# Grouping the output products of two recurrences by the part of the array they use, with one accumulation per PSUM bank and head pair

## The chip, the cores and the metric

The kernel runs on one core of one Trainium2 chip. The metric is device time in microseconds (us) of one execution. Before the change three runs gave a median of 1396.98 us (1395.22 to 1398.71).

## The reference, cut to what matters

The model has two layers, each a mixer and a SwiGLU feed-forward part, over 512 tokens of width 1024 in float32. The mixer of the first layer holds both recurrences of the title: RWKV-7 (8 heads of 64) and gated linear attention, GLA (4 heads, keys of 64, values of 128). The second layer's mixer is attention; it is not touched.

```python
def rwkv7_recurrence(r, w, k, v, a, b):
    def step(S, inp):
        r_t, w_t, k_t, v_t, a_t, b_t = inp
        sa = jnp.einsum('bhvk,bhk->bhv', S, a_t)
        S = S * w_t[:, :, None, :] + sa[..., None] * b_t[:, :, None, :] + v_t[..., None] * k_t[:, :, None, :]
        return S, jnp.einsum('bhvk,bhk->bhv', S, r_t)
...
def gla_chunked(q, k, v, log_a):                 # chunks of 64 tokens
...
    o_intra = jnp.einsum('bhncs,bhnse->bhnce', jnp.where(causal, scores, 0.0), v)
...
    o_inter = jnp.einsum('bhncd,nbhde->bhnce', q_dec, S_prev)
    return (o_intra + o_inter).reshape(Bsz, H, T, dv)
```

Both are computed chunk by chunk: a token's output is a sum of what comes from its own chunk of 64 tokens and what comes from the state S at the start of that chunk.

## The kernel before

Everything is kept transposed, channels on partitions and the 512 tokens in the free dimension. The large projections are done in three float32r matmuls each (`mm3`, L99 to L101); the matrices of the recurrences are plain float32, and each such product stands in the trace as two PE records, here called passes. The tile framework orders the instructions of each engine when the program is built; nothing is reordered at run time except what the engines do themselves.

GLA (`gla`). For each of 4 heads one PSUM bank `po` holds 128 value channels by 512 tokens. For each of 4 pairs of chunks (128 tokens) L398 multiplies v by the masked scores: 128 rows of the array (contraction over the pair's 128 tokens) and 128 columns. For each of 7 chunks (the first has no state) L402 adds S times the decayed queries: contraction over 64 key channels, so 64 rows and 128 columns. In the profile the two carry `128*128` and `64*128`. They are issued pair by pair: one L398, then the one or two L402 of that pair. Then ACT squares the bank (L406), PE sums (L410), ACT and DVE form the inverse root, PE spreads it (L416). Between the heads stand pieces of the first RWKV projections as filler.

RWKV (`rwkv_out`). A chunk of 128 channels is two heads; there are four of them (c = 0 to 3), and below they are called blocks, to keep them apart from chunks of tokens. Each is a generator, and `interleave` steps the generators in turn, the next one starting five steps after the last. A block does: triangular solves (L620, L627, L634), Gram products (L655, L657), state increments (L668), then the state recurrence: six steps of one PE product (L677) and one DVE addition (L678), then the output. The output bank `py` takes, for each of 8 token chunks and each of the 2 heads, L687 (contraction over 128, output to 64 partitions: `128*64`) and, except for the first chunk, L690 (contraction over 64 rows of that head, output to the same 64 partitions: `64*64`). The order is L687, L690 for the first head, L687, L690 for the second, then the next chunk: 16 of the one and 14 of the other per block. Then ACT squares and scales the bank (L692, L695), PE sums the squares (L700), ACT takes the root (L702), PE adds the gate product (L709, L710), ACT spreads the inverse root into `rb` (L705), PE transposes it (L714), DVE and POOL finish. The products L677 work on the whole array (`128*128`).

A second solve, for the last block alone, runs on DVE beside blocks 0 and 1: pairs L594 and L596, a transposition (L598), and copies by ACT (L603). The output projection of the GLA half (`mm3` into `pd`) is filler between the blocks.

Of the kernel before, what the change touches and what calls it, by code (L numbers as in the profile page):

```python
# [16 lines left out]
P = 128  # L17
# [38 lines left out]
def bank(g, use="pb"):  # L56
    use = use if use in g.pbufs else "pb"
    return g.ps.tile([P, 512], F32, name=use, bufs=g.pbufs[use])


def dbank(g):
    return bank(g, "pd")
# [41 lines left out]
def form_a(g, out, src, hi, lo):  # L104

    nk = src.shape[-1] // P
    step = g.wn // P
    k0 = 0
    while k0 < nk:
        n = min(step, nk - k0)  # L110
        if nk - k0 > n and nk - k0 < 2 * n:
            n = (nk - k0 + 1) // 2
        whi, wlo = load_split(g, src[:, k0 * P:(k0 + n) * P])
        for i in range(n):
            s = slice(i * P, i * P + P)
            mm3(g.nc, out, whi[:, s], wlo[:, s], hi[:, k0 + i], lo[:, k0 + i], k0 + i == 0, k0 + i == nk - 1)
        k0 += n
# [107 lines left out]
CH = 64  # L225
NQ = T // CH
# [89 lines left out]
def gla(g, m0, gp, v, tail, tailw, ob):  # L316

    nc, ap = g.nc, g.ap
    one = gp.tile([P, 1], F32, name="one", bufs=1)
    nc.vector.memset(one, 1.0)  # L320
    eps = gp.tile([P, 1], F32, name="eps5", bufs=1)
    nc.vector.memset(eps, 1e-5)
    dv = gp.tile([P, 1], F32, name="dv", bufs=1)
    nc.vector.memset(dv, 1.0 / P)

    def flat(t):
        return t.rearrange("p q t -> p (q t)")

    qd, ki, kx, eb, en, kd = ({} for _ in range(6))
    for j in range(2):  # L330
        pz = bank(g)
        nc.tensor.matmul(pz, lhsT=tailw[32:48, j * P:j * P + P], rhs=tail[32:48], start=True, stop=True)
        z = gp.tile([P, T], F32, name="z")
        cb = g.cols["gla_ba"] + j
        nc.scalar.activation(z, pz, AF.Identity, bias=g.vec[:, cb:cb + 1])
        e = gp.tile([P, T], F32, name="e")
        nc.vector.scalar_tensor_tensor(e, z, -1.0, z, op0=ALU.mult, op1=ALU.max)
        nc.scalar.activation(e, e, AF.Exp, scale=-1.0)
        nc.scalar.activation(e, e, AF.Ln, bias=one)
        nc.vector.scalar_tensor_tensor(e, z, 0.0, e, op0=ALU.min, op1=ALU.subtract)  # L340
        L = gp.tile([P, NQ, CH], F32, name="L")
        nc.vector.tensor_tensor_scan(flat(L), m0.reset, e, 0.0, ALU.mult, ALU.add)
        kd[j] = gp.tile([P, NQ, CH], F32, name="kd")
        nc.gpsimd.tensor_tensor(kd[j], L[:, :, CH - 1:CH].broadcast_to([P, NQ, CH]), L, op=ALU.subtract)
        eb[j] = gp.tile([P, NQ, CH], F32, name="eb")
        nc.scalar.activation(eb[j], L, AF.Exp, scale=1.0 / 16)
        en[j] = gp.tile([P, NQ, CH], F32, name="en")
        nc.scalar.activation(en[j], L, AF.Exp, scale=-1.0 / 16)
        nc.scalar.activation(kd[j], kd[j], AF.Exp, scale=1.0 / 16)
    for j in range(2):  # L350
        pq, pk = dbank(g), dbank(g)
        form_a(g, pk, ap["win"][14 + j], g.xhi, g.xlo)
        form_a(g, pq, ap["win"][12 + j], g.xhi, g.xlo)
        kx[j] = gp.tile([P, T], F32, name="kx")
        nc.vector.tensor_mul(kx[j], pk, g.rstd)
        ki[j] = gp.tile([P, T], F32, name="ki")
        nc.gpsimd.tensor_mul(ki[j], kx[j], flat(en[j]))
        nc.vector.tensor_mul(kx[j], kx[j], flat(kd[j]))
        qd[j] = gp.tile([P, T], F32, name="qd")
        nc.vector.tensor_mul(qd[j], pq, g.rstd)  # L360
        nc.vector.scalar_tensor_tensor(qd[j], qd[j], 0.125, flat(eb[j]), op0=ALU.mult, op1=ALU.mult)
    S, sc = {}, {}
    for j in range(2):
        pt = bank(g)
        for m in range(4):
            nc.tensor.transpose(pt[:, m * P:m * P + P], kx[j][:, m * P:m * P + P], g.ident)
        kt = gp.tile([P, 4, P], F32, name="kt")
        nc.scalar.copy(kt.rearrange("p m f -> p (m f)"), pt)
        for hp in range(2):
            rows = slice(64 * hp, 64 * hp + 64)  # L370
            psc = bank(g)
            for m in range(4):
                s = slice(m * P, m * P + P)
                nc.tensor.matmul(psc[:, s], lhsT=ki[j][rows, s], rhs=qd[j][rows, s], start=True, stop=True)
            sc[j, hp] = gp.tile([P, 4, P], F32, name="sc", bufs=4)
            nc.vector.tensor_tensor(sc[j, hp], psc.rearrange("p (m t) -> p m t", m=4),
                                    m0.lmask.unsqueeze(1).broadcast_to([P, 4, P]), op=ALU.mult)
        S[j] = gp.tile([P, NQ, P], F32, name="S")
        nc.gpsimd.memset(S[j][:, 0], 0.0)
        pkv = []  # L380
        for e in range(2):
            pkv.append(bank(g).rearrange("p (m d) -> p m d", m=4))
            r = slice(64 * e, 64 * e + 64)
            for m in range(4):
                for hp in range(2):
                    h = 2 * j + hp
                    nc.tensor.matmul(pkv[e][64 * hp:64 * hp + 64, m], lhsT=kt[r, m, 64 * hp:64 * hp + 64],
                                     rhs=v[r, m, h * P:h * P + P], start=True, stop=True)
        for q in range(NQ - 1):
            nc.vector.scalar_tensor_tensor(S[j][:, q + 1], S[j][:, q], eb[j][:, q, CH - 1:CH], pkv[q % 2][:, q // 2],  # L390
                                           op0=ALU.mult, op1=ALU.add)
    for h in range(4):
        j, hp = h // 2, h % 2
        rows = slice(64 * hp, 64 * hp + 64)
        po = bank(g)
        for m in range(4):
            s = slice(m * P, m * P + P)
            nc.tensor.matmul(po[:, s], lhsT=v[:, m, h * P:h * P + P], rhs=sc[j, hp][:, m], start=True, stop=False)  # L398
            for q in (2 * m, 2 * m + 1):
                if q:  # L400
                    t = slice(q * CH, q * CH + CH)
                    nc.tensor.matmul(po[:, t], lhsT=S[j][rows, q], rhs=qd[j][rows, t], start=False, stop=q % 2 == 1)  # L402
        o = gp.tile([P, T], F32, name="o")
        cn = g.cols["gla_norm"] + h
        sq = gp.tile([P, T], F32, name="sq")
        nc.scalar.activation(sq, po, AF.Square)  # L406
        nc.scalar.mul(o, po, g.vec[:, cn:cn + 1])
        pc = bank(g)
        for b in range(4):
            nc.tensor.matmul(pc[:, b:b + 1], lhsT=sq[:, b * P:b * P + P], rhs=dv, start=True, stop=True)  # L410
        rn = gp.tile([P, 4], F32, name="rn")
        nc.scalar.activation(rn, pc[:, :4], AF.Sqrt, bias=eps)
        nc.vector.reciprocal(rn, rn)
        pr = bank(g)
        for b in range(4):
            nc.tensor.transpose(pr[:, b * P:b * P + P], rn[:, b:b + 1].broadcast_to([P, P]), g.ident)  # L416
        nc.vector.tensor_mul(o, o, pr)
        nc.sync.dma_start(ob[h], o)
# [187 lines left out]
def rwkv_out(g, m0, st, sp, c, zeros):  # L606

    nc = g.nc
    use = f"o{c % 2}"
    no, G = zeros[c % 2]  # L610
    for e in range(2):
        rows = slice(64 * e, 64 * e + 32)
# [30 lines left out]
    qt = sp.tile([P, T], F32, name="qt", bufs=2)  # L643
# [3 lines left out]
    for e in range(2):  # L647
        er = slice(64 * e, 64 * e + 64)
        pe = bank(g, use).rearrange("p (x m f) -> p x m f", x=2, f=CH)
        for m in range(4):  # L650
            q = 2 * m + e
            for hp in range(2):
                ih, i = m // 2, 2 * (m % 2) + hp
                hr = slice(64 * hp, 64 * hp + 64)
                nc.tensor.matmul(pe[hr, 0, m], lhsT=st.r[er, ih, c, i, CH:], rhs=st.bk[er, c, q, hr],  # L655
                                 start=True, stop=True)
                nc.tensor.matmul(pe[hr, 1, m], lhsT=st.r[er, ih, c, i, CH:], rhs=st.gr[er, e, ih, c, i],  # L657
                                 start=True, stop=True)
        for hp in range(2):
            hr = slice(64 * hp, 64 * hp + 64)  # L660
# [3 lines left out]
    for q in range(NQ):  # L664
        m, e = q // 2, q % 2
        for hp in range(2):
            hr = slice(64 * hp, 64 * hp + 64)
            nc.tensor.matmul(ph[hr, q], lhsT=st.bk[:, c, q, hr], rhs=st.fv[:, e, m // 2, c, 2 * (m % 2) + hp],  # L668
                             start=True, stop=True)
    H = sp.tile([P, NQ, CH], F32, name="H", bufs=2)  # L670
    nc.scalar.copy(H, ph)
    S = sp.tile([P, NQ, CH], F32, name="S", bufs=2)
# [7 lines left out]
    py = bank(g, use)  # L680
    for q in range(NQ):
        m, e = q // 2, q % 2
        t = slice(q * CH, q * CH + CH)
        for hp in range(2):
            ih, i = m // 2, 2 * (m % 2) + hp
            hr = slice(64 * hp, 64 * hp + 64)
            nc.tensor.matmul(py[hr, t], lhsT=st.fv[:, e, ih, c, i], rhs=st.gr[:, e, ih, c, i],  # L687
                             start=True, stop=q == 0)
            if q:
                nc.tensor.matmul(py[hr, t], lhsT=S[hr, q], rhs=qt[hr, t], start=False, stop=True)  # L690
    sq = sp.tile([P, T], F32, name="sq", bufs=1)
    nc.scalar.activation(sq, py, AF.Square)  # L692
    y = sp.tile([P, T], F32, name="y", bufs=2)
# [14 lines left out]
    s = slice(c * P, c * P + P)  # L708
# [493 lines left out]
```

## Time and profile before

| | |
|---|---|
| median of 3 runs | 1396.98 us |
| profiled execution | 1397.71 us, span 1395.9 us |
| PE busy | 1358.7 us, 97% of the span, 6868 records |
| DVE, ACT, POOL busy | 699.9, 563.8, 185.5 us |
| mean granted PE clock | 0.969 of full speed |

Where in the span: GLA's outputs stand from 90.8 to 119.6 us, the RWKV blocks' outputs between 286.2 and 374.6 us, and from 420 us on there are only the feed-forward parts and the attention layer. A timeline row gives start and length; since consecutive passes overlap in the array, the time a row costs is the distance from its start to the start of the row behind it. The clock column reads 1.00 at 2.4 GHz and 0.50 at 1.2 GHz.

### The profile page before, as it was taken

What the parts mean: (1) busy time and instruction counts of PE and PEld (TensorE: products, weight loads), DVE (VectorE), ACT (ScalarE), POOL (GpSimd) and SP (SyncE); (2) the same over time, 40 slices, a digit from 0 to 9 for tenths busy, and PEclk for the clock granted to TensorE, in tenths of its full rate; (3) what the DMA queues carried; (4) which work ended last, traced back from release to release, by engine and by line L of the source; (5) the groups of instructions that cost most, each with busy time, mean ns of one, the idle gap of its engine ahead of it and who ended that gap; (6) DMA issues with size and microseconds to landing.
All of it is one profiled execution on the core that took longest, in us unless ns stands there. A gap on an engine that the chain in (4) does not pass through costs nothing.

```text
span 1395.9 us, 17759 instructions
## 1 busy us (share of the span) xinstructions
PE 1358.7 (97%) x6868; PEld 1111.0 (80%) x6868; DVE 699.9 (50%) x1223; ACT 563.8 (40%) x949; POOL 185.5 (13%) x167
## 2 busy tenths in 40 slices
PE   8999999799999999999999999999999999999996
PEld 6788777688787888888888888888888888888885
DVE  7563869843255343343434327898643433344332
ACT  6534774422244232222323436777532322233232
POOL 3011111200141111001111100000111110011111
PEclk9999999868799999999999999999999999999998
DMA  6122222402264432333323432221223323432231
GB/s 191 59 74 63 77 69 90 142 8 76 92 219 142 152 98 72 107 113 94 102 74 93 124 91 76 62 61 46 76 91 105 91 75 99 118 102 91 78 95 69
DMA packets 50848, 131.11 MB, mean 94 GB/s; under 512 B 5859, under 2 KB 6243, under 8 KB 50764
## 3 DMA queue, kind: packets, MB, share of 16 engines
q1 hardware_dynamic: 49900, 128.81, 30.6%
q8 instruction: 54, 0.88, 0.3%
q10 hardware_dynamic: 864, 1.17, 0.2%
q14 instruction: 30, 0.25, 0.1%
HBM read 121.22 MB, written 11.36 MB: 95 GB/s over the span
## 4 chain that ended last, share of the span: by engine, by line
PE 90%; DVE 6%; ACT 2%; issue 1%; DMA 0%; DVEq 0%; ACTq 0%
PE pd L100 24%; PE pd L101 24%; PE pd L99 24%; PE po L1001 1%; PE o L687 1%; PE o L690 1%; PE o L634 1%; PE o L627 1%; DVE wlo L89 1%; PE sc L976 1%; PE sc L977 1%; DVE tmp L594 1%; PE pb L402 1%; PE o L620 1%; PE o L101 1%
## 5 line engine op out<-in xcount | busy, mean ns | idle before, releaser
L88 ACT CAST whi<-wraw 128x1024 fp32r<-128x1024 f32 (+2 forms) x248 | 215.6, 871 | 545.8 <-PE pd L100 339.4
L101 PE MATMUL pd<-xhi,wlo 128*128 128x512 f32 x1064 | 421.2, 396 | 0.0
L99 PE MATMUL pd<-xhi,whi 128*128 128x512 f32 x1064 | 420.1, 395 | 0.9 <-ACT xhi L180 0.9
L100 PE MATMUL pd<-xlo,whi 128*128 128x512 f32 x1064 | 420.2, 395 | 0.0
L89 DVE TENSOR_TENSOR wlo<-wraw,whi 128x1024 fp32r<-128x1024 f32 (+2 forms) x248 | 256.3, 1036 | 143.9 <-ACT whi L88 143.4
L99 PEld LDWEIGHTS pd<-xhi,whi 128*128 128x128 f32 x1064 | 201.0, 189 | 42.7 <-ACT xhi L180 1.3
L100 PEld LDWEIGHTS pd<-xlo,whi 128*128 128x128 f32 x1064 | 201.2, 189 | 41.7 <-issue 0.2
L101 PEld LDWEIGHTS pd<-xhi,wlo 128*128 128x128 f32 x1064 | 201.2, 189 | 41.2 <-DVE wlo L89 0.2
L215 POOL TENSOR_TENSOR hlo<-h,hhi 128x512 fp32r<-128x512 f32 x44 | 66.7, 1516 | 547.4 <-ACT hhi L214 547.4
L100 PE MATMUL pd<-hlo,whi 128*128 128x512 f32 x352 | 136.9, 389 | 0.0
L99 PE MATMUL pd<-hhi,whi 128*128 128x512 f32 x352 | 136.9, 389 | 0.0
L101 PE MATMUL pd<-hhi,wlo 128*128 128x512 f32 x352 | 136.9, 389 | 0.0
L211 DVE TENSOR_TENSOR ut<-pd,rstd 128x512 f32<-128x512 f32 x44 | 30.4, 691 | 147.1 <-PE pd L101 147.1
L208 DVE TENSOR_TENSOR gt<-pd,rstd 128x512 f32<-128x512 f32 x44 | 30.4, 691 | 124.5 <-PE pd L101 122.4
L101 PEld LDWEIGHTS pd<-hhi,wlo 128*128 128x128 f32 x352 | 66.1, 188 | 13.8
L99 PEld LDWEIGHTS pd<-hhi,whi 128*128 128x128 f32 x352 | 66.1, 188 | 13.8
L100 PEld LDWEIGHTS pd<-hlo,whi 128*128 128x128 f32 x352 | 66.1, 188 | 13.6
L221 DVE TENSOR_TENSOR xT<-pd,xT 128x512 f32<-128x512 f32 x32 | 22.1, 691 | 67.3 <-PE pd L101 67.3
L149 POOL TENSOR_TENSOR ssum<-nsq,ssum 128x512 f32<-128x512 f32 x26 | 37.2, 1430 | 81.7 <-ACT nsq L145 81.4
L981 ACT ACTIVATE s<-s,mn 128x384 f32<-128x384 f32 (+3 forms) x64 | 35.7, 559 | 21.4 <-DVE mn L978 20.8
L214 ACT CAST hhi<-h 128x512 fp32r<-128x512 f32 x44 | 27.4, 623 | 37.1 <-DVE h L213 37.1
L957 POOL TENSOR_TENSOR qst<-q,qst 64x512 fp32r<-64x512 f32 x8 | 12.9, 1611 | 168.0 <-DVE qst L955 168.0
(327 smaller groups left out, 1686.1 us busy)
## 6 DMA issues: line engine op xcount, KB each, us to landing
wraw<-in_gate SPq DMA_DIRECT2D x44, 512.0 KB, 3.7
wraw<-in_up SPq DMA_DIRECT2D x44, 512.0 KB, 3.6
wraw<-in_down SPq DMA_DIRECT2D x32, 384.0 KB, 3.1
wraw<-in_win SPq DMA_DIRECT2D x40, 256.0 KB, 2.7
wraw<-in_down SPq DMA_DIRECT2D x32, 320.0 KB, 2.9
wraw<-in_wqk SPq DMA_DIRECT2D x16, 512.0 KB, 3.7
xT<-in_xT SPq DMA_DIRECT2D x16, 256.0 KB, 3.6
wraw<-in_wout SPq DMA_DIRECT2D x16, 256.0 KB, 3.9
```

What stands on the lines that cost most here:

```text
L88: nc.scalar.copy(hi, raw)
L89: nc.vector.tensor_sub(lo, raw, hi.bitcast(F32))
L99: nc.tensor.matmul(out, lhsT=lhi, rhs=rhi, start=start, stop=False)
L100: nc.tensor.matmul(out, lhsT=lhi, rhs=rlo, start=False, stop=False)
L101: nc.tensor.matmul(out, lhsT=llo, rhs=rhi, start=False, stop=stop)
L149: (nc.vector if c in fast else nc.gpsimd).tensor_add(ss, sq, first if c == 1 else ss)
L208: nc.vector.tensor_mul(gt, pg, rstd)
L211: nc.vector.tensor_mul(ut, pu, rstd)
L214: nc.scalar.copy(hhi[:, n], h)
L215: nc.gpsimd.tensor_sub(hlo[:, n], h, hhi[:, n].bitcast(F32))
L221: nc.vector.tensor_add(g.xT[:, j], pd, g.xT[:, j])
L981: nc.scalar.activation(s[:, m, :L], s[:, m, :L], AF.Exp, bias=mn[:, m:m + 1], scale=-1.0, accum_out=sm[:, m:m + 1])
```

## The change

Both outputs issue the same products into the same banks in another order: first all that don't read S, then all that do. The flags follow: `start` on the first product of a bank (in the RWKV case of each head's half of it), `stop` on the last.

```diff
         po = bank(g)
         for m in range(4):
             s = slice(m * P, m * P + P)
-            nc.tensor.matmul(po[:, s], lhsT=v[:, m, h * P:h * P + P], rhs=sc[j, hp][:, m], start=True, stop=False)
-            for q in (2 * m, 2 * m + 1):
-                if q:
-                    t = slice(q * CH, q * CH + CH)
-                    nc.tensor.matmul(po[:, t], lhsT=S[j][rows, q], rhs=qd[j][rows, t], start=False, stop=q % 2 == 1)
+            nc.tensor.matmul(po[:, s], lhsT=v[:, m, h * P:h * P + P], rhs=sc[j, hp][:, m], start=m == 0, stop=False)
+        for q in range(1, NQ):
+            t = slice(q * CH, q * CH + CH)
+            nc.tensor.matmul(po[:, t], lhsT=S[j][rows, q], rhs=qd[j][rows, t], start=False, stop=q == NQ - 1)
...
             nc.tensor.matmul(py[hr, t], lhsT=st.fv[:, e, ih, c, i], rhs=st.gr[:, e, ih, c, i],
-                             start=True, stop=q == 0)
-            if q:
-                nc.tensor.matmul(py[hr, t], lhsT=S[hr, q], rhs=qt[hr, t], start=False, stop=True)
+                             start=q == 0, stop=False)
+    for q in range(1, NQ):
+        t = slice(q * CH, q * CH + CH)
+        for hp in range(2):
+            hr = slice(64 * hp, 64 * hp + 64)
+            nc.tensor.matmul(py[hr, t], lhsT=S[hr, q], rhs=qt[hr, t], start=False, stop=q == NQ - 1)
```

On PE, one GLA head before (the first; L398 reads scores `sc` and `v`, L402 reads queries `qd` and state `S`):

```order
L387 MATMUL pb<-v,kt 64x128 x16
L398 MATMUL pb<-sc,v 128x128
L402 MATMUL pb<-qd,S 128x64
L398 MATMUL pb<-sc,v 128x128
L402 MATMUL pb<-qd,S 128x64 x2
L398 MATMUL pb<-sc,v 128x128
```

The same head on PE with the change (L401 is the line that was L402):

```order
L387 MATMUL pb<-v,kt 64x128 x16
L398 MATMUL pb<-sc,v 128x128 x4
L401 MATMUL pb<-qd,S 128x64 x7
L100 MATMUL pd<-xlo,whi 128x512
L101 MATMUL pd<-xhi,wlo 128x512
```

The products of one kind stand together; the projection's matmuls behind them keep their place.

On PE, the start of the last block's output before (`gr`, `xT`: the products without S; `qt`, `S`: those with it; `G`: the recurrence step):

```order
L101 MATMUL pd<-xhi,wlo 128x512
L99 MATMUL pd<-xhi,whi 128x512
L677 MATMUL o_3189<-S,G_2486 128x64
L687 MATMUL o_3192<-gr,xT 64x64 x3
L690 MATMUL o_3192<-qt,S 64x64
L687 MATMUL o_3192<-gr,xT 64x64
```

The same block on PE with the change (line numbers behind L402 shift by one or two: L676 was L677, L686 was L687, L692 was L690):

```order
L101 MATMUL pd<-xhi,wlo 128x512
L99 MATMUL pd<-xhi,whi 128x512
L676 MATMUL o_3189<-S,G_2486 128x64
L686 MATMUL o_3192<-gr,xT 64x64 x16
L692 MATMUL o_3192<-qt,S 64x64 x14
L100 MATMUL pd<-xlo,whi 128x512
```

Thirty products that changed kind at almost each step became two runs.

On PE, block 0's output before, around the end, where other blocks' work is woven in (`bkt`: state increments of block 1; `r`, `ga`: the first solve of block 2):

```order
L668 MATMUL o_2714<-xT,bkt 64x64 x16
L687 MATMUL o_2741<-gr,xT 64x64
L690 MATMUL o_2741<-qt,S 64x64
...
L687 MATMUL o_2741<-gr,xT 64x64
L620 MATMUL o_2781<-r,ga 128x128 x3
L677 MATMUL o_2738<-S,G_2486 128x64
L690 MATMUL o_2741<-qt,S 64x64
```

The same place on PE with the change:

```order
L686 MATMUL o_2741<-gr,xT 64x64 x16
L692 MATMUL o_2741<-qt,S 64x64 x2
L667 MATMUL o_2714<-xT,bkt 64x64 x16
L692 MATMUL o_2741<-qt,S 64x64 x10
L619 MATMUL o_2781<-r,ga 128x128 x3
L676 MATMUL o_2738<-S,G_2486 128x64
L692 MATMUL o_2741<-qt,S 64x64 x2
```

The work of the other blocks is woven in at the same places; within the block's own products only the order changed.

No engine issues an instruction more or fewer. On SP some 35 transfers around the output projection (weights, parts and the reload of xT) change places with each other, and DVE and ACT follow with their weight splits.

## Rows read from the trace of the kernel before

**Rows 1.** Busy time by stretch, core 0: engines, then granted clock, DMA share, GB/s.
```profile
289.80:313.30 23.50, 23.50 (x121) 18.61 (x122) 7.86 (x26) 7.47 (x12) 0.15 (x1) 0.50 0.05 12
...
323.90:334.00 10.10, 10.10 (x49) 8.59 (x48) 1.14 (x3) 2.66 (x5) 0.00 (x0) 0.50 0.37 115
...
347.80:354.30 6.50, 6.50 (x33) 5.04 (x34) 0.21 (x1) 2.73 (x7) 1.27 (x1) 0.50 0.02 3
...
354.30:371.70 17.40, 17.36 (x183) 12.82 (x180) 7.98 (x20) 4.79 (x10) 2.57 (x2) 0.99 0.24 77
371.70:381.80 10.10, 10.10 (x33) 6.68 (x32) 0.20 (x1) 2.06 (x4) 1.26 (x1) 0.50 0.54 182
sum 95.60, PE 95.56 PEld 73.73 DVE 31.50 ACT 24.78 POOL 8.46; mean PE 11.94 PEld 9.22 DVE 3.94 ACT 3.10 POOL 1.06
```

**Rows 2.** Chain of waits, 286.2 to 374.6 us, shares by line.
```profile
by line: PE o L687 19.8%; PE o L690 19.7%; PE o L620 8.6%; PE o L627 6.4%; PE o L634 6.1%; PE o L677 5.6%; PE o L710 4.6%; PE o L668 4.6%; PE o L700 4.2%; PE o L709 4.2%; PE o L655 3.1%; PE pd L101 2.3%; PE o L714 2.2%; PE o L657 2.1%; PE p
```

**Rows 3.** Timeline of PE, block outputs: start, length, line, output, rows*columns of the array.
```profile
290.10 0.47 PE L687 MATMUL o<-gr,xT 128*64 128x64 f32 x2
...
366.58 0.33 PE L690 MATMUL o<-qt,S 64*64 64x64 f32 x2
366.84 0.33 PE L687 MATMUL o<-gr,xT 128*64 128x64 f32 x2
...
374.18 0.47 PE L690 MATMUL o<-qt,S 64*64 64x64 f32 x2
374.58 0.79 PE L100 MATMUL pd<-xlo,whi 128*128 128x512 f32 x1
```

**Rows 4.** Timeline of PE, runs of one tile shape.
```profile
177.08 1.14 PE L565 MATMUL pb<-xT,ga 64*64 64x64 f32 x30
...
290.90 1.97 PE L668 MATMUL o<-xT,bkt 128*64 128x64 f32 x32
...
358.69 1.15 PE L668 MATMUL o<-xT,bkt 128*64 128x64 f32 x32
```

**Rows 5.** Timeline of PE, recurrence step L677 between two kinds of neighbours.
```profile
279.25 0.35 PE L677 MATMUL o<-S,G 128*128 128x64 f32 x2
279.42 2.16 PE L634 MATMUL o<-w,ga 128*128 128x128 f32 x8
...
283.18 0.43 PE L677 MATMUL o<-S,G 128*128 128x64 f32 x2
283.54 0.34 PE L655 MATMUL o<-bkt,r 64*64 64x64 f32 x4
```

**Rows 6.** Timeline of PE, second GLA head.
```profile
102.56 0.43 PE L402 MATMUL pb<-qd,S 64*128 64x64 f32 x2
102.92 0.49 PE L398 MATMUL pb<-sc,v 128*128 128x128 f32 x2
103.34 0.66 PE L402 MATMUL pb<-qd,S 64*128 64x64 f32 x4
103.93 0.49 PE L398 MATMUL pb<-sc,v 128*128 128x128 f32 x2
```

**Rows 7.** Busy time by stretch, behind the first GLA head.
```profile
95.50:102.00 6.50, 6.50 (x21) 5.33 (x21) 0.87 (x2) 2.58 (x4) 0.00 (x0) 0.50 0.01 3
```

**Rows 8.** Timeline of DVE and ACT, end of the second solve; PE behind it.
```profile
304.91 1.25 DVE L598 STREAM_TRANSPOSE xt<-xl 128x1024 f32<-128x1024 f32 x1
...
308.09 0.62 ACT L705 COPY rb<-rn 128x512 f32<-128x512 f32 x1
...
311.94 1.06 PE L714 MATMUL o<-ident,rb 128*128 128x128 f32 x4
```

**Rows 9.** DMA issues on the page: KB each, us to landing.
```profile
wraw<-in_wout SPq DMA_DIRECT2D x16, 256.0 KB, 3.9
```

## The prediction

> **What bounds the kernel now.** I read the busy time by stretch first, since the change touches two short places only. In the 95.6 us from 286.2 to 381.8 PE is busy for 95.56 [rows 1]: what PE saves there, the kernel saves, until another engine is late. DVE is busy for 31.5 and ACT for 24.8 of it. The same rows show a second thing: four stretches, 50.2 us together, stand at a granted clock of 0.50, the lower of its two levels. Then the chain of waits over 286.2 to 374.6: L687 and L690 hold 39.5% of 88.4 us, so 34.9 us for 120 products [rows 2]. Then the timeline: at the upper level a product that follows one of the other kind costs 0.26 us (366.58 to 366.84), at the lower one 0.40 (374.18 to 374.58) [rows 3].
>
> What such a product should cost stands in the runs of one shape. L668 has the shape of L687, alternates between the same two halves of the columns, and does 32 passes in 1.15 us, 0.036 a pass; L565 has the shape of L690 and does 30 in 1.14, 0.038 a pass [rows 4]. So two passes cost 0.07 in a run and 0.26 in the alternation: 0.19 is the price of a switch. That it is the shape and not the accumulation onto a region just written is shown by L677, which accumulates onto nothing: two passes cost 0.17 among neighbours of its own shape (279.25 to 279.42) and 0.36 among 64*64 ones (283.18 to 283.54) [rows 5]. The difference is again 0.19.
>
> **The change part by part.** No instruction is added or taken away; only PE's order matters.
>
> GLA heads. One L398 and two L402 take 102.92 to 103.93, 1.01 us. Four passes of L402 take 0.59 (103.34 to 103.93) and two 0.36 (102.56 to 102.92), so a pass in a run costs 0.115, and six of them 0.69 [rows 6]. The pair of switches costs 0.32. Three such pairs go per head, the switch from the four L398 to the seven L402 stays: 0.95 per head, **3.8 us** for four.
>
> Block outputs. A grouped output is 32 passes at 0.036, 28 at 0.038 and one switch of 0.19: 2.4 us, 9.6 for four. Where other blocks' work is woven in, a run is cut: in block 0 by L667 and by L619 with L676, in block 1 by L676, in block 2 by transposes and by solves; about ten more switches, 1.9 us. So 34.9 become 11.5: **23.4 us**. Bounds: nothing off if the blocks keep their switches elsewhere, 25 if the cuts are free.
>
> The clock. Each of the four stretches at 0.50 begins inside an alternating output and lasts into the work behind it [rows 1]. About 40 of the 120 products stand at the spacing of 0.40, the first at 290.10 and the last at 374.18 [rows 3]: 16 us of the 50.2. The other 34.2 us are solves, gates and projection at half speed. The same work costs less at the upper level: L668 takes 1.15 there and 1.97 here [rows 4], 0.58 of the time; the levels themselves stand 2 to 1, and I take 0.55, since passes with more columns wait less for weights. If the falls go with the alternation, 45% of 34.2 is **15.4 us**. The 6.5 us at 0.50 behind the first GLA head [rows 7] give **2.9 us** in the same way. No row shows what the clock does after a grouped output; the bounds are 0 and 20.4 (half of 40.7). I take a value near the upper one, because L668's run, the nearest row in shape, is dense (0.036 a pass), and because what is at 0.50 today follows alternation in all five places.
>
> What is late next. With PE faster, its order makes it wait for others. The place is block 0's transposes of `rb` (L714, today at 311.94 [rows 8]). PE's work up to there is 25.7 us today, 9.4 of it outputs; at the upper level 16.3 x 0.55 = 9.0, and 3.2 for the output with its cuts: reached at 286.2 + 12.2 = 298.4. DVE has 7.9 us of work in that stretch [rows 1]; some 4 us of it are the last solve steps and the state's additions, in turn with PE's steps, behind a copy of the state that can start at about 289.5. I let them take 6, to 295.8. The transposition L598, the three copies of ACT and the spread L705 then follow one another; today from 304.91 to 308.71, 3.8 us [rows 8]. So `rb` is there at 299.6, and PE waits 1.2 us. I add as much again for the other blocks, where squares and copies stand between PE's steps: **minus 2.5 us**, bounds 0 and 10 (if every block waits twice as long).
>
> Costed at nothing: SP's new order. Transfers take 54% of the DMA engines' time in the stretch where they bunch [rows 1], and the weights are held three tiles ahead. If that cover is gone, one late tile costs at most its landing time of 3.9 us [rows 9]. That S of the last chunk must be there is no new wait: its product was the last of the bank before as well.
>
> A rule that speaks against the change: the two heads' L692 now stand next to each other, with different halves of the rows and one bank. The trace has that case: L565 alternates between the two halves of the rows and writes one bank, to different partitions, at 0.038 a pass [rows 4]. The Trainium skill, TensorEngine Tiling (Array Packing), section Gotcha 1: PSUM Pressure, says that different row tiles cannot access the same PSUM bank at the same time. By the rule the 28 passes would stand one behind the other; by the row they don't, and the sum goes by the row.
>
> Sum: 3.8 + 23.4 + 15.4 + 2.9 - 2.5 = 43.0 us. The profiled execution took 1397.7 (its span of 1395.9 and 1.8 around it), so 1354.7; it lies 0.7 above the median, which makes **1354 us**.
>
> **The rivals.**
> 1. The falls of the clock stay, since PE's work behind the outputs (sums of squares with two columns, solves) is thin too. For it: block 0's stretch at 0.50 lasts 23.5 us, through such work. Against it: the same kinds of work stand at 0.99 between 354.3 and 371.7 [rows 1]. Then only 3.8 + 23.4 come, 1370; with the outputs at the lower level as well (0.062 a pass, so 18.9 for four in place of 11.5) 1377.
> 2. Waits take the place of the work: the solve on DVE and the chain of squares, root and spread on ACT bound each block. Each has 8 us or less of work in the longest stretch [rows 1], so it takes the 10 us of the bound above: 1362.
> 3. Passes that differ in the half of the rows don't overlap. The nearest row for passes on one half is L402's 0.115 [rows 6]: 28 x (0.115 - 0.038) = 2.2 us per block, 8.6 in all: 1363. This is what the Trainium skill's rule above would do.
> 4. The switch is not what costs, and the order gives nothing: 1397. Against it stand rows 3 to 5.
> 5. Slower: PE, no longer filled by the alternation, waits so often that the clock stays at 0.50 over the whole stage. Of the 60.7 us that are no outputs 26.5 are at the upper level now; they would become 48, the 34.2 stay, and the outputs take 18.9: 101 for 95.6. The three later GLA heads (three times 1.01 and a first pair, 3.7 us, now) would take 5.0: together 9 us more, 1406. Against it: 45.4 us of the stage are at the upper level now, with waits in their midst. It decides from about four fifths of the work at the lower level.
>
> **How the numbers follow.** Forecast 0.62, rival 1 0.20, rival 2 0.09, rival 3 0.04, rival 4 0.03, rival 5 0.02. The forecast's own range is 1347 (no cuts, no waits, all that is at 0.50 in half its time: 3.8 + 25.3 + 20.4 off) to 1363. The range of 1345 (by the 2 us that the runs lie below their median) to 1373 takes in rivals 2 and 3 and half of rival 1; some 0.17 is left out. Faster by over 0.3% (what a measurement can tell here from no change, 4 us): 0.95; within: 0.03; slower: 0.02.
>
> **What would show it.** Right: L398 and L401 of a head in some 2.7 us without an L398 between L401; sixteen L686 in 1.2 us and fourteen L692 in 1.1, neighbours 0.07 apart; no stretch at 0.50 that begins inside an output; 286.2 to 381.8 shrunk from 95.6 to about 59; from 420 us on, nothing but a shift. Wrong: the clock still falls behind the outputs (rival 1); PE idle before L716, L702 or L633 for more than a few us (rival 2); L692 spaced at 0.2 (rival 3). The forecast is wrong if the stage shrinks by less than 30 us.

## The result, and the profile after

The changed kernel takes 1354.1 us (median of 4 runs, 1350.58 to 1354.56) against 1397.2 (median of 4 runs beside it): ratio 0.9687, 95% interval 0.9667 to 0.9707. The forecast was 1354. The profiled execution took 1354.56 us, with a span of 1352.8; PE is busy for 1314.1 us of it, 44.6 less than before, and DVE, ACT and POOL for within 1.2 us of what they were.

Busy time by stretch, columns as in [rows 1]: GLA's outputs; the 13 us ahead of block 0's output and through most of it; the rest of the blocks; what follows.

```profile
90.80:113.90 23.10, 23.10 (x154) 20.64 (x152) 5.98 (x14) 6.73 (x12) 0.00 (x0) 0.93 0.18 57
272.70:286.00 13.30, 13.30 (x156) 12.02 (x158) 7.47 (x24) 1.92 (x6) 0.00 (x0) 0.50 0.01 1
286.00:338.90 52.90, 51.40 (x618) 41.32 (x614) 27.87 (x74) 24.53 (x48) 7.82 (x6) 1.00 0.31 95
338.90:400.00 61.10, 60.20 (x266) 47.66 (x266) 33.29 (x44) 29.29 (x45) 21.18 (x15) 1.00 0.54 173
```

The four stretches at 0.50 of [rows 1] (called falls of the clock below) are gone: from 286 us to the end of the blocks, and on to 400, the clock is at its upper level. One stretch of 13.3 us at 0.50 remains; it begins before block 0's output. Shorter ones stood ahead of the blocks in the kernel before too, where no output alternates:

```profile
211.20:214.50 3.30, 3.30 (x10) 2.55 (x9) 1.79 (x7) 0.86 (x3) 0.00 (x0) 0.50 0.28 82
255.60:262.30 6.70, 5.42 (x25) 5.45 (x26) 4.42 (x7) 4.51 (x8) 2.65 (x2) 0.50 0.33 98
265.80:269.20 3.40, 3.40 (x18) 3.40 (x17) 3.18 (x6) 0.89 (x3) 1.74 (x2) 0.50 0.91 263
279.50:282.80 3.30, 3.30 (x21) 2.99 (x21) 2.05 (x7) 1.33 (x4) 0.00 (x0) 0.50 0.00 0
```

From the first output to the last transposes the blocks took 96.1 us (286.24 to 382.38), and now 57.5 (281.36 to 338.85).

The chain of waits over 281.4 to 338.9 us, against [rows 2]:

```profile
by line: PE o L692 8.2%; PE o L686 8.0%; PE o L619 7.1%; PE o L633 6.5%; PE o L676 6.4%; PE o L712 5.5%; PE o L667 5.2%; PE o L711 4.8%; PE pd L99 4.7%; PE pd L100 4.7%; PE pd L101 4.7%; PE o L702 4.4%; PE o L654 3.9%; PE o L626 3.4%; PE o 
```

The output products held 39.5% and hold 16.2%, of a shorter stretch.

The timeline of PE, against [rows 3, 4, 6]: one GLA head, then block 0's output at the lower level, the one long wait, and the last block's output.

```profile
98.07 1.06 PE L398 MATMUL pb<-sc,v 128*128 128x128 f32 x8
99.06 1.77 PE L401 MATMUL pb<-qd,S 64*128 64x64 f32 x14
100.76 0.50 PE L101 MATMUL pd<-xhi,wlo 128*128 128x512 f32 x1
...
281.36 1.98 PE L686 MATMUL o<-gr,xT 128*64 128x64 f32 x32
283.26 0.48 PE L692 MATMUL o<-qt,S 64*64 64x64 f32 x4
283.67 1.97 PE L667 MATMUL o<-xT,bkt 128*64 128x64 f32 x32
...
295.79 0.66 PE L716 MATMUL o<-ident,rb 128*128 128x128 f32 x4 [1.21 <-ACT rb L707]
...
331.86 0.39 PE L99 MATMUL pd<-xhi,whi 128*128 128x512 f32 x1
332.09 0.39 PE L676 MATMUL o<-S,G 128*128 128x64 f32 x2
332.41 1.15 PE L686 MATMUL o<-gr,xT 128*64 128x64 f32 x32
333.49 1.03 PE L692 MATMUL o<-qt,S 64*64 64x64 f32 x28
334.46 0.50 PE L100 MATMUL pd<-xlo,whi 128*128 128x512 f32 x1
```

A head takes 2.69 us (98.07 to 100.76) where it took 3.68. The last output takes 2.05 (332.41 to 334.46) where it took 8.4; by distances from row to row, PE's waits left out, the four outputs took 35.0 us and take 10.5. PE waits 1.21 us for `rb` at 295.79.

### The profile page after: what moved, and what is told of

Same layout as the page of the kernel before. It is cut to its first block, busy times and chain, and to the rows that moved or that the text cites. A ratio compares the mean times of both kernels' runs of the same rounds, so it can differ in the third digit from the quotient of the medians.

```text
span 1352.8 us, 17760 instructions
## 1 busy us (share of the span) xinstructions
PE 1314.1 (97%) x6868; PEld 1081.0 (80%) x6868; DVE 698.8 (52%) x1223; ACT 563.3 (42%) x949; POOL 186.7 (14%) x167
## 4 chain that ended last, share of the span: by engine, by line
PE 89%; DVE 6%; ACT 3%; issue 1%; DMA 0%; POOL 0%; DVEq 0%; ACTq 0%
PE pd L100 25%; PE pd L99 25%; PE pd L101 25%; PE po L1003 1%; DVE wlo L89 1%; PE o L633 1%; DVE tmp L593 1%; PE sc L978 1%; PE sc L979 1%; DVE xl L595 1%; PE o L99 1%; PE o L101 1%; PE o L100 1%; PE pb L401 1%; PE pt L999 0%
## 5 line engine op out<-in xcount | busy, mean ns | idle before, releaser
L99 PE MATMUL pd<-xhi,whi 128*128 128x512 f32 x1064 | 418.4, 394 | 0.9 <-ACT xhi L180 0.9
L101 PE MATMUL pd<-xhi,wlo 128*128 128x512 f32 x1064 | 418.7, 394 | 0.0
L99 PEld LDWEIGHTS pd<-xhi,whi 128*128 128x128 f32 x1064 | 199.9, 188 | 42.3 <-ACT xhi L180 1.3
L101 PEld LDWEIGHTS pd<-xhi,wlo 128*128 128x128 f32 x1064 | 199.9, 188 | 41.2 <-DVE wlo L89 0.2
L99 PE MATMUL pd<-hhi,whi 128*128 128x512 f32 x352 | 136.9, 389 | 0.0
L101 PE MATMUL pd<-hhi,wlo 128*128 128x512 f32 x352 | 136.9, 389 | 0.0
L99 PEld LDWEIGHTS pd<-hhi,whi 128*128 128x128 f32 x352 | 66.1, 188 | 13.8
L101 PEld LDWEIGHTS pd<-hhi,wlo 128*128 128x128 f32 x352 | 66.1, 188 | 13.8
```

What stands on the lines that cost most here:

```text
L99: nc.tensor.matmul(out, lhsT=lhi, rhs=rhi, start=start, stop=False)
L101: nc.tensor.matmul(out, lhsT=llo, rhs=rhi, start=False, stop=stop)
```

## The experiments

Times stand against runs of the kernel before on the same chip. Their medians are 1397.4 for each half alone, the flags and the dense products; 1395.3 for the grouping by chunk, the products head by head, and -80 and -300; and 1398.9 for the lagged order, the single tiling, and the two kernels side by side.

**One half of the change each.** First GLA's grouping alone (L687 to L690 as before).

> The grouping in the GLA heads alone; the RWKV blocks keep the old order. Theory (each part is worth what its own stretch shows in the changed kernel's trace, and the two parts don't meet): 5.6 us off, 1391.6; GLA's end near 113.9 us, the four falls of the clock after the block outputs stay, 286 to 382 us keeps its 95 to 96 us. Rival (the head start of GLA is absorbed by later waits on DVE or on transfers): the time is that of before, 1397. Rival (the GLA grouping also lifts the clock later): below 1385.

Measured: 1391.9 us, ratio 0.9953 (0.992 to 0.9987). Busy time by stretch:

```profile
90.80:114.50 23.70, 23.70 (x187) 21.03 (x182) 6.66 (x17) 7.54 (x14) 0.00 (x0) 1.00 0.17 56
271.90:299.10 27.20, 27.20 (x197) 22.63 (x195) 9.88 (x34) 4.16 (x10) 0.00 (x0) 0.50 0.03 11
...
364.00:381.10 17.10, 17.10 (x54) 11.48 (x53) 3.02 (x5) 3.68 (x7) 1.50 (x2) 0.50 0.33 107
```

GLA's part is as expected, 5.5 us (the interval allows 1.8 to 11.2), and four falls stay in the ungrouped blocks. The first of them begins at 271.9, ahead of block 0's output (280.89), and runs on through it.

Then the blocks' grouping alone (L398 to L402 as before).

> The grouping in the RWKV blocks alone; GLA keeps the old order. Theory (as above): about 37.5 us off, 1359.7, with the four falls of the clock gone and the stretch from the first output to the last transposes near 57.5 us; GLA's four heads at 3.7 to 3.8 us each and its fall behind the first head (95.5 to 102) still there. Rival (both parts are needed for the clock): one or more of the four falls stays and the time lies above 1365.

Measured: 1355.6 us, ratio 0.9689 (0.9637 to 0.974): 41.8 us off, 4 more than expected.

```profile
284.40:340.00 55.60, 54.09 (x689) 43.78 (x689) 30.96 (x83) 24.84 (x48) 7.51 (x6) 1.00 0.29 91
90.80:123.00 32.20, 32.20 (x176) 25.77 (x173) 6.30 (x16) 8.78 (x16) 0.00 (x0) 0.90 0.13 42
```

The blocks run at 1.00 from their first output on. GLA has a fall, but of 10.2 us from 116.3 on, not behind the first head. About 4 us are what the 13.3 us stretch at 0.50 costs, which the changed kernel's first profile had ahead of the blocks and this one does not have: from the recurrence step at its place (270.64 there, 277.50 here) to the first output it is 10.7 us there and 6.9 here.

**The flags without the order.**

```diff
-  ... start=True, stop=q == 0)          # L687
+  ... start=q == 0, stop=False)
-  ... start=False, stop=True)           # L690
+  ... start=False, stop=q == NQ - 1)
```

> The old alternating order of the products in both recurrences, with the new flags: one accumulation per bank and head pair. It tells the accumulation from the order. Theory (the price is the switch of the array's tiling): nothing changes, 1397, L686 and L690 still 0.26 us apart at the upper level and the four falls stay. Rival (closing and opening an accumulation at each chunk costs): a part of the 43 us comes, below 1390, and the spacing shrinks.

Measured: 1398.4 us, ratio 1.0003 (0.997 to 1.0036). One accumulation per bank is worth nothing that these runs can tell, and four falls stay. Three begin inside outputs (10.1, 6.7 and 17.1 us); the first begins ahead of block 0's output (288.46). Its row, then the timeline of PE, one block's output:

```profile
279.50:306.70 27.20, 27.18 (x197) 22.66 (x195) 9.85 (x34) 4.19 (x10) 0.00 (x0) 0.50 0.04 11
```

```profile
367.61 0.33 PE L687 MATMUL o<-gr,xT 128*64 128x64 f32 x2
367.87 0.33 PE L690 MATMUL o<-qt,S 64*64 64x64 f32 x2
368.12 0.33 PE L687 MATMUL o<-gr,xT 128*64 128x64 f32 x2
```

**Is it the tiling, or adding onto columns just written?** Alternation has both. Two kernels part them. The first keeps the alternation, takes the flags of one accumulation, and puts the product with S one chunk behind:

```diff
-    for q in range(NQ):              # product without S of q, then with S of q
+    for q in range(NQ + 1):          # product without S of q, then with S of q - 1
```

> The kernel before with the blocks' products still alternating between the two tilings, but the product with S runs one chunk behind, so it adds onto columns that were written four products earlier instead of just now. Theory (the switch): spacing stays at 0.26, falls stay, 1392 to 1398. Rival (adding onto columns just written): spacing falls towards 0.07, 1360 to 1370.

Measured: 1396.0 us, ratio 0.9979 (0.9954 to 1.0005). Timeline of PE, then the longest fall:

```profile
367.47 0.33 PE L687 MATMUL o<-gr,xT 128*64 128x64 f32 x2
367.73 0.33 PE L691 MATMUL o<-qt,S 64*64 64x64 f32 x2
367.98 0.33 PE L687 MATMUL o<-gr,xT 128*64 128x64 f32 x2
```
```profile
291.20:315.00 23.80, 23.80 (x125) 18.80 (x124) 8.40 (x28) 7.47 (x12) 0.23 (x1) 0.50 0.04 12
```

The spacing is 0.26 still, and four falls begin inside the outputs (47.6 us at 0.50). The second keeps order and flags and takes the switch away:

```diff
+    for hp in range(2):
+        hr = slice(64 * hp, 64 * hp + 64)
+        nc.scalar.copy(Sz[hr, hp], S[hr, 1:])       # Sz: zeros in the other head's rows
...
-   nc.tensor.matmul(py[hr, t], lhsT=S[hr, q], rhs=qt[hr, t], start=False, stop=True)
+   nc.tensor.matmul(py[hr, t], lhsT=Sz[:, hp, q - 1], rhs=qt[:, t], start=False, stop=True)
```

> The kernel before with its alternating order and its flags, but the products with S of the blocks read a copy of S that holds zeros in the other head's rows (two copies by ACT per block, 448 columns each), so that L693 has the same tiling (128 rows by 64 columns) as L687. Order kept, switch taken away. Theory (the switch of the tiling is the price): products 0.07 to 0.08 us apart, outputs near 2.3 us without cuts, the four falls go; RWKV's gain of 38 to 42 us less 4 x about 1 us for the copies ahead of each output: 1357 to 1362. Rival (what costs is to accumulate onto columns that were just written): spacing stays at 0.26, the falls stay, about 1400. Both in part: between.

Measured: 1361.1 us, ratio 0.9728 (0.967 to 0.9787). Timeline of PE inside block 0's output, then busy time by stretch:

```profile
297.80 0.27 PE L693 MATMUL o<-qt,Sz 128*64 128x64 f32 x2
297.86 0.22 PE L690 MATMUL o<-gr,xT 128*64 128x64 f32 x1
297.91 0.22 PE L693 MATMUL o<-qt,Sz 128*64 128x64 f32 x1
297.92 0.27 PE L690 MATMUL o<-gr,xT 128*64 128x64 f32 x2
```
```profile
290.00:347.00 57.00, 55.43 (x710) 45.26 (x707) 31.87 (x86) 28.34 (x53) 7.46 (x6) 1.00 0.25 81
```

In the old order, onto the same columns, the pattern now repeats every 0.115 us (297.80 to 297.91, one product of each kind) where it took 0.52. The four outputs take 10.2 us, and no fall is left from the first output on. So the price is the switch of the tiling.

**Does the clock fall for the switches, or because PE has little to do between them?** The alternation of the flags' kernel with a dense product of zeros between any two of its products of one head:

```diff
             if q:
+                nc.tensor.matmul(py[hr], lhsT=m0.zero, rhs=dense, start=False, stop=False)   # 512 columns
                 nc.tensor.matmul(py[hr, t], lhsT=S[hr, q], ...)
```

> As the kernel with the old order and the new flags, but in the blocks' outputs a product of zero weights with 512 columns stands before each L690, in L686's tiling and on the same bank (16 per block, two of them ahead): it adds zeros, some 28 us of dense PE work (64 times two passes of 0.22 us), and takes no switch away. Theory (the clock falls because PE works sparsely in the alternation): the four falls go although the alternation stays; the outputs then cost 120 x 0.26 + 28 = 59 us at the upper level, the work behind them gains its 15 us: 1397 + 28 - 21 = 1404. Rival (switching the tiling lowers the clock, however dense the work): the falls stay, the added work is partly at the lower level, 1425 to 1440. Rival (the falls come from the thin work behind the outputs): falls begin behind the outputs, not in them, 1415 to 1425.

Measured: 1428.3 us, ratio 1.0214 (1.0146 to 1.0283). Timeline of PE, then busy time by stretch:

```profile
287.18 0.59 PE L693 MATMUL o<-bkt,zero 128*64 128x512 f32 x1
287.61 1.09 PE L668 MATMUL o<-xT,bkt 128*64 128x64 f32 x30
...
333.61 0.32 PE L694 MATMUL o<-qt,S 64*64 64x64 f32 x2
333.86 0.33 PE L690 MATMUL o<-gr,xT 128*64 128x64 f32 x2
334.03 1.02 PE L693 MATMUL o<-bkt,zero 128*64 128x512 f32 x2
334.98 0.32 PE L694 MATMUL o<-qt,S 64*64 64x64 f32 x2
```
```profile
285.60:430.00 144.40, 142.81 (x890) 78.79 (x890) 42.27 (x95) 34.36 (x62) 12.20 (x10) 1.00 0.25 78
```

By its time alone this is the value of the first rival. The trace speaks for the theory: the clock is at 1.00 from the first output on, with the switches all there. The added work was mis-sized: a pass of 512 columns takes 0.43 us (287.18 to 287.61), not 0.22, so 64 x 0.86 = 55 us came in; 1397 + 55 - 1428 leaves 24 us gained, where 21 were expected. The switches cost what they did: from one L694 to the next 1.37, of which the dense product is 0.86 and the two others 0.14, so 0.37 for two switches. So the switches alone don't bring the falls: as many of them, with dense products between, leave the clock up, also through the thin work behind the outputs.

**Is a switch a fixed price?** The changed kernel, grouped per chunk in the blocks: two products without S, two with.

```diff
-    for q in range(1, NQ): ...       # all products with S behind all without
+        if q:
+            for hp in range(2): ...  # both heads' products with S behind both without, chunk by chunk
```

> GLA as in the changed kernel; in the RWKV blocks the products are grouped per chunk of 64 tokens: two L686, then two products with S, and so on, so about 14 switches for one per output, where the old order had 28. Theory (a fixed price of 0.19 us per switch, plus the clock): 13 more switches x 0.19 x 4 = 10 us at the upper level, 1364; if the falls of the clock come back with the half-sparse order, 8 to 16 us more, up to 1380. Rival (the price is for any alternation, not per switch): the time of the old order in the blocks, 1391. Rival (pairs are enough): 1354.

Measured: 1356.1 us, ratio 0.9712 (0.9657 to 0.9768). Timeline of PE:

```profile
336.27 0.34 PE L686 MATMUL o<-gr,xT 128*64 128x64 f32 x4
336.54 0.33 PE L691 MATMUL o<-qt,S 64*64 64x64 f32 x4
336.80 0.50 PE L100 MATMUL pd<-xlo,whi 128*128 128x512 f32 x1
```
```profile
279.40:340.00 60.60, 59.38 (x686) 46.99 (x685) 30.99 (x83) 24.89 (x48) 7.48 (x6) 1.00 0.28 84
```

A group of two products takes 0.265 us, as a single one did. Its two products lie in different parts of the array, and the next experiment shows that such products overlap. The four outputs take 15.9 us, 6.6 above those of the changed kernel at the upper level (9.3): 0.14 for each of 48 more switches (13 in place of 1 per output), not 0.19. No fall comes back. The time is 8 us below the theory's 1364: that was reckoned with 0.19 and from 1354, with the 13.3 us stretch at 0.50, which is 3.4 us long in this profile.

**Do passes on different halves of the rows overlap?**

```diff
-    for q in range(1, NQ):
-        for hp in range(2):
+    for hp in range(2):
+        for q in range(1, NQ):       # the products with S, head by head
```

> The changed kernel, but each output's products with S go through all seven chunks of the one head and then of the other, so neighbours have the same half of the array's rows. Theory (passes that alternate between the halves overlap, those of one half don't): L692's spacing rises from 0.034 a pass to between 0.06 and 0.115 (the pace of L402 in one head), 28 x 0.03 to 0.08 x 4 = 3 to 9 us more, 1357 to 1363. Rival (the halves do not overlap on one bank, as rival 3 of the prediction had it; or a pass has one price anyway): no change, 1354.

Measured: 1352.7 us, ratio 0.9685 (0.964 to 0.973); the time tells nothing, the trace does:

```profile
300.52 1.66 PE L692 MATMUL o<-qt,S 64*64 64x64 f32 x28
302.11 0.43 PE L676 MATMUL o<-S,G 128*128 128x64 f32 x2
```

From start to start 28 passes take 1.59 us (300.52 to 302.11) where they take 0.97 (333.49 to 334.46): 0.057 a pass on one half, 0.035 in alternation. They do overlap, and the four outputs are 2.4 us longer than in a profile of the changed kernel at the upper level. That the time is still short goes with what the blocks alone showed: no stretch at 0.50 between 272 and 286 us.

This also parts the price of 0.19. A product by itself on one half needs two passes of 0.057, 0.11 us; in the alternation it took 0.26. So 0.14 to 0.15 of that is the switch, as in the grouping by chunk. The other 0.05 (0.19 less 0.14) is the overlap with the neighbour on the other half, which a product loses when the next one has another tiling.

**The wait ahead of block 0, and a faster version.** The stretch at 0.50 that was left stood behind a wait of PE of 1.96 us. Two kernels let DVE do the state's copy before more of the second solve:

```diff
-        with g.tc.high_priority(-15):
+        with g.tc.high_priority(-80):     # in the other kernel -300
             solve(g, st, slv, [RC - 1])
```

> The changed kernel with the second solve's vector work at a lower priority (-80 for -15), so that DVE does block 0's state copy (L672) and sums into G before more pairs of the solve. It aims at PE's wait of 1.96 us near 270 us, which stands ahead of the one stretch at 0.50 that is left before the blocks' outputs (272.7 to 286.0, 13.3 us). Theory (the wait brings the fall): wait and fall go, 2 + 13.3 x 0.45 = up to 8 us off, 1346 to 1350. Rival (the fall comes from the thin work of the recurrence steps there): the wait goes, the fall stays, 1352. Rival (the solve's pairs are then late for block 2 and 3): PE waits there instead, 1354 or more.

> As the last, with -300: nearly all the solve's vector work gives way to the blocks'. Same theories; here the late solve is likelier: PE idle before block 2's first products (L619) by several us, 1354 to 1365; without that 1346 to 1350.

Measured: 1347.3 us, ratio 0.9654 (0.9608 to 0.97), and 1350.8 us, 0.9683 (0.9631 to 0.9734). The waits of PE in the first of the two:

```profile
PE o L676 <- DVE S L672: 1.0, 2, 0.7
```
```profile
264.00:290.00 26.00, 25.27 (x368) 22.12 (x367) 22.36 (x64) 9.73 (x21) 2.10 (x2) 1.00 0.10 34
```

(The waits' columns are us in total, times, and the longest.) Of 1.96 us 0.7 is left, and the fall is gone. So it looked as if the wait brought the fall. With -300 PE waits 0.8 us for block 2's first products, not several; its time lies just above the 1346 to 1350 expected for that. To see whether the 7 us are the priority's, both kernels ran again side by side.

> The changed kernel itself, beside the others on one chip, to see whether the stretch at 0.50 at 272.7 to 286.0 us, which stood in its first profile and not in the three related kernels' profiles, is a property of its order or of the one execution. Theory (it hangs on small differences of time): a shorter fall or none there, 1348 to 1355. Rival (the order brings it): the same stretch again, 1354.

> The changed kernel with the second solve's vector work at -80, beside it on the same chip, for an interval between the two. If the 7 us of the earlier comparison are real: 1347 against 1354, intervals of the two ratios apart. Rival (they were the state of the clock ahead of block 0 in the executions timed): both within 3 us.

Measured: 1350.7 us for the changed kernel, ratio 0.9662 (0.9625 to 0.9698), and 1349.7, 0.9647 (0.9609 to 0.9684), with -80. The two can't be told apart. The changed kernel's timeline of PE and its busy time by stretch, second profile:

```profile
270.72 0.41 PE L676 MATMUL o<-S,G 128*128 128x64 f32 x2 [1.96 <-DVE S L672]
...
277.65 1.15 PE L686 MATMUL o<-gr,xT 128*64 128x64 f32 x32
```
```profile
250.00:335.00 85.00, 77.05 (x965) 64.97 (x966) 56.11 (x145) 36.40 (x75) 14.37 (x12) 0.98 0.33 103
```

The same order, the same wait of 1.96, and no fall behind it: block 0's output runs in 1.15 us. The fall at 272.7 us is not a property of the order, and the wait does not bring it alone. The kernel before has the same wait, and the 3.3 us at 0.50 from 279.5 on behind it:

```profile
277.98 0.41 PE L677 MATMUL o<-S,G 128*128 128x64 f32 x2 [1.96 <-DVE S L673]
```

Of all eleven profiles with this wait eight have a fall within 2 us behind it, 3.4 to 27.2 us long; the other three (this one, the blocks alone, the products head by head) have none, and the three with a wait of 0.7 have none either. The times point the same way: of the changed kernel's ten runs five took 1348.8 to 1351.7 us, at a mean granted clock of 0.990 to 0.993, and five 1353.9 to 1355.7, at 0.985 to 0.987; the nine with -80 all took 1351.3 or less, at 0.989 or more. A shorter wait may make the fall rarer; these runs don't show it. The lower priority removes 1.2 us of waiting, and no version here beats the changed kernel by what these runs can tell.

## Why the prediction was right

- **PE bounds the stretch, and the switch costs 0.19 us.** Right as the difference per product, and shown from both sides: with the alternation kept it costs the same (lagged, dense), and with the switch taken away the old order repeats in 0.115 us. Rival 4 falls with it. But the 0.19 holds two things that the prediction did not part: some 0.14 for the switch and 0.05 for the lost overlap of the two halves.
- **GLA heads, 3.8 us and 2.9 for the clock.** 3.3 us in the outputs (three heads at 2.7 to 2.8, the last at 3.38, partly at 0.50); GLA ends 5.6 earlier, 119.51 against 113.90, for 6.7 predicted. The difference: the 6.5 us at 0.50 went, but 3.4 us at 0.50 came from 108.6 on, in the last head's output and ahead of it. In the profile of GLA's grouping alone, with no fall there, GLA takes 21.5 us (92.01 to 113.52) where it took 28.7, so 7.2 less.
- **Block outputs, 34.9 to 11.5 us.** 10.5, with block 0's at the lower level; 9.3 in the second profile, where all is at the upper one. There they are 2.34, 2.37, 2.54 and 2.04: the uncut one costs 2.04 where 2.4 was put, the cuts of the others 1.1 together where 1.9 was.
- **The clock, 15.4 us less 2.5 of waits.** The blocks' other work with its waits shrank from 61.1 us to 47.0: 14.1, for 12.9. Waits are 1.5 of it (1.21 before L716, where 1.2 was predicted, and 0.3 before L676); that other blocks would wait as much was too much. The 1.2 came out although both of its terms were 1.0 us too late: in the second profile, at the upper level throughout, PE is there 11.2 us behind the first output and `rb` at 12.4, for 12.2 and 13.4 predicted. Rival 1 is refuted: the same sums of squares, gates and solves run at 1.00. (In one of the eight profiles with grouped blocks, that of -300, 3.4 us at 0.50 stand among them, from 299.4 on.) Over all runs the mean granted clock is 0.979 at most where the blocks' products alternate with nothing between, and 0.981 at least in the other kernels. Rival 2's 10 us of waits are 1.5.
- **Rows overlap in one bank.** L692 alternates between the halves at 0.035 us a pass and needs 0.057 on one half, so rival 3 is wrong, and the rule weighed there (the Trainium skill, TensorEngine Tiling (Array Packing), section Gotcha 1: PSUM Pressure: different row tiles cannot access one bank at the same time) does not hold here, for products that write different partitions of the bank.
- **The sum, 43.0.** 43.1 between the two first profiled executions. That agreement is better than its reason, and in part luck: GLA gave 1.1 less than predicted, the outputs 1.1 and the rest of the blocks 1.2 more, and 1.2 were lost between GLA and the blocks and behind them. The 13.3 us at 0.50 ahead of the blocks hide some 6 us of gain, as the second profile (1348.78) shows; of that fall the prediction said nothing. Its reason for the clock was also too simple. It says that what was at 0.50 before followed alternation in all five places, but the four other stretches of the kernel before (211 to 283 us, 16.7 us together) follow no alternating output; three of them begin in or just behind waits of PE of 4.8, 2.1 and 2.0 us. The alternation's four falls went as forecast; those ahead of the blocks come and go without it.
- **From 420 us on a shift only.** From the last transposes to the end it is 0.43 us longer than before.

What stays open is why the stretch at 272 us stands at 0.50 in some executions and not in others with the same order.

## What to carry to other kernels

In a row of small products on TensorE, look for changes of tiling (rows*columns in the timeline) from one to the next, and compare the distance between starts with that in a run of one tiling: here 0.26 us against 0.07. Order by tiling as far as the data allow, or give all products one tiling by padding with zeros. Neighbours should lie in different parts of the array, so that they overlap; runs of two such products already gave most of the gain here, 6.6 us less in the outputs than long runs. Then read the granted clock: the alternating stretches cost twice here, once in themselves and once in the work behind them, an estimated 15 us of the 43.

## What the runs showed of the hardware beyond that

- The clock's falls differ between executions of one kernel: 13.3 us at 0.50 ahead of block 0 in one profile of the changed kernel and none there in the other, 5.8 us apart in time, and its ten runs fall into two groups some 4 us apart. A difference of that size between two kernels needs several executions before a cause is named.
- A pass of 512 columns of plain f32 takes 0.43 us, a pass of the split products (L99 to L101), with as many columns, 0.23 (331.86 to 332.09). The dense kernel's price was wrong by that factor.
- In GLA, where falls also come and go, the grouped order stood at 0.50 for 0 to 3.4 us in its eight profiles, and the alternating one for 6.8 to 20.4 in its six.
